# Copies for the weight sums, one behind every second weight load, and accumulating transfers head by head

## The chip, the cores and the metric

The kernel runs on one core of a Trainium2 chip. The metric is device time in microseconds (us) of one execution, the median of several. Engines are named as in the profile: PE (TensorE, matmuls), PEld (its weight loads), DVE (VectorE), ACT (ScalarE), POOL (GpSimd) and SP (SyncE, which issues DMAs). DMAs issued by POOL run in the queue q0, those of SP in q1.

## The reference

A layer of a model: 512 rows of 1024, float32. After a norm, one wide product (`w_in`) makes the inputs of two branches. Branch A (8 heads) is a gated delta rule with a convolution ahead of it; branch B (4 heads) is a retention with a rotary embedding. Both end in a norm, a gate and a product, are mixed and added, and a two-layer network of width 4096 follows.

```python
def hybrid_layer(x, ...):
    proj = rmsnorm(x, n_mix_pre) @ w_in
    qa, ka, va, za, beta_logit, a_dt, qb, kb, vb, gb, gate_a, gate_b = _split_cols(proj, IN_SIZES)
    ...
    oa = chunk_gated_delta_rule(qa, ka, va, beta, g)
    ya = (rmsnorm(oa, norm_a) * silu(za)) @ w_br_a
    qb, kb = rotary(qb), rotary(kb) * B_DK ** -0.5
    ob = chunk_retention(qb, kb, vb)
    yb = (rmsnorm(ob, norm_b) * silu(gb)) @ w_br_b
    x = x + rmsnorm((sigmoid(gate_a) * ya + sigmoid(gate_b) * yb) @ w_out, n_mix_post)
    return x + rmsnorm(square(relu(rmsnorm(x, n_mlp_pre) @ w_up)) @ w_down, n_mlp_post)
```

For each of the four heads of branch B, `vb` and `gb` are 512 columns each of `w_in`.

## The kernel before

Every float32 product is made of three matmuls: each operand is split into a high part and the rest (`mm3`). Weights come in chunks of 128 x 1024 (512 KB). A chunk is loaded by SP into a buffer `raw`, ACT writes its high part `whi` (L104), DVE the rest `wlo` (L105), and PE uses both in 24 matmuls of 128x512. `raw` has two buffers, `whi` and `wlo` three each. `weights` (L85) counts all loads in `loads`; chunk i takes its buffer from `raw_pools[i % len(raw_pools)]`. So SP can issue a load only when the split of an earlier chunk has freed its buffer, and all loads are in one queue, in the order that the scheduler laid down. Each engine works its instructions off in order; a scheduler lays that order down when the kernel is built, by priorities, and `tc.issue_after(x)` puts what is issued under it behind x.

The stages that matter here:

- Branch A: in the pools `pa` and `pa2`, a loop over `g2` (four pairs of heads). Each turn has `recurrence` (a chain of small products, with its `vn` on ACT, L637), `values_queries` for the next pair, `gated`, the partial product `ya_partial` of the pair before, and `gated_features`, which transposes the rows `vt` on PE (L211) and splits them on ACT and DVE (`og`, L194, L195).
- Branch B: in the pool `pb`, a loop over the heads h. `scores(h)` has the Q and K products, the rotary embedding (`rope`, `ro`, `qr`, `kr`) and the scores with a decay table `dec`; `outputs(h)` computes values and gates (`values_and_gates`). In the turn h = 0 the sums of the inputs (`feature_sums`: `full`, `xsum`), `ya_partial(3)` and the gate of branch A stand between the two. `pb`'s tiles lie in memory that `pa2` had used, so the first use of each waits until `pa2`'s users are done.
- `values_and_gates` makes two products with common inputs out of seven quarter products instead of eight. For that it needs four sums of blocks of `w_in` for each head, 128 x 4 x 512 each. They are made in DRAM, ahead of time, by DMAs: `BlockSums` copies four blocks of 1 MB into four tiles `sums` (L121) and then adds to each of them with accumulating DMAs of 512 KB (L127). Two of the four sums have another one as their addend, so these accumulates must wait for it. For this SP later loads 8 chunks per head from `sums` (L136).

Before the change `vg_pair` (L702) issues all of this on POOL's queue for two heads at a time, in the turns `g2` = 1 and 2, behind POOL's last instruction of that turn (`pool_marks`): 8 copies, then 16 accumulates, of which those of the third block go first. The extra `raw` buffers `ych` in `pb` (L915) come into use ahead of head 0, so that load 61, the first of the two for head 0's Q, is the first to use one.

Of the kernel before, what the change touches and what calls it, by code (L numbers as in the profile page):

```python
# [15 lines left out]
ALU = mybir.AluOpType  # L16
# [10 lines left out]
OFF_QB, OFF_KB, OFF_VB, OFF_GB = 6160, 7184, 8208, 10256  # L27
# [33 lines left out]
def hybrid_block_kernel(ctx: ExitStack, tc: tile.TileContext, a: dict, out: bass.AP):  # L61
    nc = tc.nc
    x_d = a["x"][0]
    w_in = a["w_in"][0]
# [4 lines left out]
    ring = ctx.enter_context(tc.tile_pool(name="ring", bufs=3))  # L69
    raw_pools = [(ring, "raw")]  # L70
    loads = itertools.count()
    act = ctx.enter_context(tc.tile_pool(name="act", bufs=2))
    sm = ctx.enter_context(tc.tile_pool(name="sm", bufs=2))
    psm = ctx.enter_context(tc.tile_pool(name="psm", bufs=4, space=PSUM))
# [10 lines left out]
    def weights(src, k0, nk, c0, ncols, keep=None):  # L85

        n = nk * ncols
        i = next(loads)
        pool, tag = raw_pools[i % len(raw_pools)]
        raw = pool.tile([P, 1024], F32, tag=tag, name="raw", bufs=2)  # L90
        nc.sync.dma_start(
            raw[:, :n].rearrange("p (k c) -> p k c", k=nk),
            src[k0 * P : (k0 + nk) * P, c0 : c0 + ncols].rearrange("(k p) c -> p k c", p=P),
        )
        return split_weights(raw, n, nk, keep, 200 if i >= 6 else 0)

    def split_weights(raw, n, nk, keep=None, ahead=200):
# [13 lines left out]
    class BlockSums:  # L111


        def __init__(self, src, c1, c2, tag):
            def block(kh, c):
                return src[4 * kh * P : 4 * (kh + 1) * P, c : c + 512].rearrange("(k p) c -> p k c", p=P)

            self.w12, self.first = block(0, c2), [block(0, c1), block(0, c1), block(1, c2), block(1, c1)]
            self.t = [dr.tile([P, 4, 512], F32, tag=f"{tag}{i}", name="sums", bufs=1) for i in range(4)]
            for t, b in zip(self.t, self.first):  # L120
                nc.gpsimd.dma_start(t, b)  # L121

        def add(self, i):

            src = (self.w12, self.t[2], self.w12, self.t[1])[i]
            for k in range(0, 4, 2):
                nc.gpsimd.dma_start(self.t[i][:, k : k + 2, :], src[:, k : k + 2, :], accum_op=ALU.add)  # L127

        def weights(self, i, ks):
            return block_weights(self.t[i - 1][:, 2 * ks : 2 * ks + 2, :])  # L130
# [306 lines left out]
    with tc.tile_pool(name="pa", bufs=1) as pa:  # L437
# [250 lines left out]
        def gated(g2, rows, pool):  # L688
            pss = token_major(w_in, x_tile, OFF_ZA + g2 * 512, 8)
            zz = pool.tile([P, 4, T], F32, tag="zz", name="zz")  # L690
            gate_rows(pss, rows, lambda t: zz[:, t, :])

        with tc.tile_pool(name="pa2", bufs=1) as pa2:
            keys(0, pa2)
            scr = base_inverse(0, pa2)
            vq = values_queries(0, pa2)
            keys(1, pa2)
            double_blocks(pa2, scr, 0)
            og = None
            vg_sums = []  # L700

            def vg_pair(h0):  # L702
                pair = [BlockSums(w_in, OFF_VB + h * 512, OFF_GB + h * 512, f"vg{h}") for h in range(h0, h0 + 2)]
                for i in (2, 0, 1, 3):
                    for sums in pair:
                        sums.add(i)
                return pair

            for g2 in range(4):
                rows = recurrence(g2, vq, pa2)  # L710
                if g2 == 0:
                    double_blocks(pa2, scr, 8)
                    scr = base_inverse(1, pa2)
                if g2 < 3:
                    vq = values_queries(g2 + 1, pa2)
                if g2 == 1:
                    double_blocks(pa2, scr, 16)
                    double_blocks(pa2, scr, 24)
                if g2 in (1, 2):
                    with tc.issue_after(pool_marks[-1].ins):  # L720
                        vg_sums += vg_pair(2 * g2 - 2)
                gated(g2, rows, pa2)
                if g2:
                    ya_partial(g2 - 1, og)
                og = gated_features(rows, lambda f: na[:, f % 2 : f % 2 + 1])
# [3 lines left out]
    with tc.tile_pool(name="pb", bufs=1) as pb_:  # L729
# [112 lines left out]

        def scores(h):
            dec = pb_.tile([P, T], F32, tag="dec", name="dec")
            nc.gpsimd.dma_start(dec, a["c_decay"][h])
            qs, ks = (pb_.tile([P, 2, 2, T], F32R, tag=nm, name=nm) for nm in ("qr", "kr"))
            qs, ks = [qs[:, 0], qs[:, 1]], [ks[:, 0], ks[:, 1]]
            rotary(feature_major(w_in, xs, OFF_QB + h * 256, 256, 8), qs)
            rotary(feature_major(w_in, xs, OFF_KB + h * 256, 256, 8), ks)
            scs = []  # L850
            for i in range(4):
                t0 = min(i * P, 256)
                n = T - t0
                ps = psx.tile([P, T], F32, tag="dl", name="dl", bufs=3)
                for kk in range(2):
                    mm3(
                        ps[:, :n],
                        [ks[j][:, kk, i * P : (i + 1) * P] for j in range(2)],
                        [qs[j][:, kk, t0:T] for j in range(2)],
                        kk == 0,  # L860
                        kk == 1,
                    )
                n2 = T - i * P
                sc = tmp("sc")
                nc.vector.tensor_tensor(sc[:, :n2], ps[:, n - n2 : n], dec[:, :n2], ALU.mult)
                sh, sl = (pb_.tile([P, n2], F32R, tag=f"s{i}{j}", name="s") for j in range(2))
                nc.scalar.copy(sh, sc[:, :n2])
                nc.vector.tensor_tensor(sl, sc[:, :n2], sh, ALU.subtract)
                scs.append((sh, sl))
            return scs  # L870
# [41 lines left out]
        def gate_product(off, half):  # L912
            return feature_major(w_in, xs, off + half * 512, 512, 8)

        raw_pools.append((pb_, "ych"))  # L915
        for h in range(4):
            scs = scores(h)
            if h == 0:
                feature_sums()
                ya_partial(3, prev)  # L920
                for half in range(2):
                    pss = gate_product(OFF_GA, half)
                    for f in range(4):
                        ta = tmp("g_t")
                        nc.scalar.activation(ta, pss[f], AF.Tanh, scale=0.5)
                        dst = acc[:, half * 4 + f, :]
                        nc.vector.scalar_tensor_tensor(dst, ta, 1.0, dst, ALU.add, ALU.mult)
                    nc.gpsimd.dma_start(ya_d[:, half * 4 : half * 4 + 4, :], acc[:, half * 4 : half * 4 + 4, :])
            else:
                for half, pss in branch_partial(w_br[1], prev, 4 * (h - 1)):  # L930
                    for f in range(4):
                        dst = accb[:, half * 4 + f, :]
                        if h == 1:
                            nc.scalar.copy(dst, pss[f])
                        else:
                            nc.vector.tensor_tensor(dst, dst, pss[f], ALU.add)
            rows = outputs(h, scs)
            prev = gated_features(rows, lambda f: nb[:, 4 * h + f : 4 * h + f + 1])

# [214 lines left out]
```

## Time and profile before

| | us |
|---|---|
| time, median of 3 runs | 1421.01 (1420.75 to 1422.48) |
| profiled execution, its own time | 1422.03 |
| its span, first to last instruction | 1420.3 |
| DVE busy | 869.8 |
| ACT busy | 613.2 |
| POOL busy | 98.9 |
| mean granted PE clock | 0.987 |

The profile is of one execution. A busy time is the union of an engine's instructions. Matmuls overlap, so that one of 0.39 us starts every 0.23 us; PE's share of the span says how long it had something in work. In the views of waits and of the timeline, brackets give the idle time of an engine ahead of an instruction and what ended it. "DMA share" is the mean busy share of the 16 DMA engines, "PEclk" the granted clock.

| DMA, kind | count | KB each | median us to landing |
|---|---|---|---|
| raw<-in_w_in_dram (SP) | 105 | 512 | 3.8 |
| raw<-in_w_br_a_dram (SP) | 16 | 512 | 6.4 |
| sums<-in_w_in_dram, copies (POOL) | 16 | 1024 | 19.6 |
| sums<-in_w_in_dram, accumulates (POOL) | 16 | 512 | 21.8 |
| sums<-sums, accumulates (POOL) | 16 | 512 | 16.9 |

### The profile page before, as it was taken

The page shows a single profiled execution, that of the slowest core. Times are in us where ns is not written, and L with a number is a line of the kernel's source. Part 1 is how long each engine was busy: PE and PEld are TensorE (multiplying, and loading weights), DVE is VectorE, ACT ScalarE, POOL GpSimd, SP SyncE. Part 2 cuts the span into 40 slices and gives each one's busy share as a digit, 9 for nine tenths or more (in the row PEclk, how much of TensorE's full clock was granted, in tenths as well). Part 3 has the DMA queues.
Part 4 walks back from the last instruction along what each step waited for, and adds up shares of the span by engine and source line. Part 5 has one row for each costly group of instructions (what it writes and reads, how often), then busy time and mean ns, then how long its engine had stood idle before and what let it go on. Part 6 is the DMA issues. An engine that isn't in the chain of part 4 may idle for free.

```text
span 1420.3 us, 17580 instructions
## 1 busy us (share of the span) xinstructions
PE 1376.5 (97%) x6670; PEld 1127.5 (79%) x6670; DVE 869.8 (61%) x1539; ACT 613.2 (43%) x1134; POOL 98.9 (7%) x152
## 2 busy tenths in 40 slices
PE   8999999999899979999999999999999999999997
PEld 6888787877787758887887888878788888888886
DVE  5599889843664467348467577475776324334445
ACT  6778564625443232254453353443354324132331
POOL 1111300233022000000000000000000000000000
PEclk8999999999999989999999999999999999999999
DMA  5232412289569733354262352542624323222321
GB/s 156 75 91 75 117 31 75 77 294 231 138 240 262 180 111 96 120 189 123 83 192 83 120 161 75 166 162 73 230 82 137 102 94 99 95 99 98 109 75 60
DMA packets 83959, 180.08 MB, mean 127 GB/s; under 512 B 5823, under 2 KB 19281, under 8 KB 83362
## 3 DMA queue, kind: packets, MB, share of 16 engines
q1 hardware_dynamic: 68560, 131.61, 29.6%
q0 software_dynamic: 14592, 46.10, 12.6%
q8 instruction: 52, 0.85, 0.2%
q10 hardware_dynamic: 722, 1.25, 0.2%
q14 instruction: 33, 0.27, 0.1%
HBM read 173.17 MB, written 39.32 MB: 150 GB/s over the span
## 4 chain that ended last, share of the span: by engine, by line
PE 80%; DVE 8%; DMA 8%; ACT 3%; issue 1%; SPq 0%; DVEq 0%; POOL 0%; ACTq 0%
PE mm L81 19%; PE mm L83 19%; PE mm L82 19%; PE mm L772 9%; DMA raw<-in_w_in_dram 5%; PE tr L211 2%; DVE wlo L105 2%; DMA raw<-in_w_br_a_dram 2%; PE dl L772 2%; ACT whi L104 1%; DVE c_y L399 1%; PE dl L81 1%; PE dl L83 1%; PE dl L82 1%; PE dl L662 1%
## 5 line engine op out<-in xcount | busy, mean ns | idle before, releaser
L105 DVE TENSOR_TENSOR wlo<-raw,whi 128x1024 fp32r<-128x1024 f32 x232 | 283.6, 1224 | 358.0 <-ACT whi L104 357.0
L104 ACT CAST whi<-raw 128x1024 fp32r<-128x1024 f32 x232 | 243.8, 1052 | 466.1 <-PE mm L82 206.6
L81 PE MATMUL mm<-actT,whi 128*128 128x512 f32 (+1 forms) x528 | 209.2, 397 | 8.5 <-ACT whi L104 5.1
L82 PE MATMUL mm<-actT,whi 128*128 128x512 f32 (+1 forms) x528 | 210.1, 398 | 1.0 <-DVE actT L245 1.0
L83 PE MATMUL mm<-actT,wlo 128*128 128x512 f32 (+1 forms) x528 | 209.5, 397 | 0.0
L81 PEld LDWEIGHTS mm<-actT,whi 128*128 128x128 f32 x528 | 101.3, 192 | 29.9 <-ACT whi L104 5.5
L82 PEld LDWEIGHTS mm<-actT,whi 128*128 128x128 f32 x528 | 101.6, 192 | 20.7 <-DVE actT L245 1.3
L83 PEld LDWEIGHTS mm<-actT,wlo 128*128 128x128 f32 x528 | 101.6, 192 | 19.1 <-DVE wlo L105 0.2
L81 PE MATMUL mm<-hn,whi 128*128 128x512 f32 (+1 forms) x288 | 105.6, 367 | 0.6 <-DVE r L1077 0.5
L82 PE MATMUL mm<-hn,whi 128*128 128x512 f32 (+1 forms) x288 | 105.4, 366 | 0.0
L83 PE MATMUL mm<-hn,wlo 128*128 128x512 f32 (+1 forms) x288 | 105.1, 366 | 0.0
L81 PE MATMUL mm<-og,whi 128*128 128x512 f32 x256 | 100.2, 392 | 3.0 <-DVE zz L362 3.0
L82 PE MATMUL mm<-og,whi 128*128 128x512 f32 x256 | 99.7, 389 | 0.0
L83 PE MATMUL mm<-og,wlo 128*128 128x512 f32 x256 | 99.6, 389 | 0.0
L81 PE MATMUL mm<-whi,actT 128*128 128x512 f32 x216 | 86.3, 399 | 0.1
L82 PE MATMUL mm<-wlo,actT 128*128 128x512 f32 x216 | 85.8, 397 | 0.0
L83 PE MATMUL mm<-whi,actT 128*128 128x512 f32 x216 | 85.5, 397 | 0.0
L772 PE MATMUL mm<-whi,xsum 128*128 128x512 f32 x256 | 80.1, 389 | 0.0
L399 DVE SCALAR_TENSOR_TENSOR c_y<-c_raw,convw,c_y 128x512 f32<-128x512 f32 x96 | 70.6, 753 | 2.9 <-ACT c_y L397 2.3
L81 PEld LDWEIGHTS mm<-hn,whi 128*128 128x128 f32 x288 | 54.3, 188 | 10.2 <-DVE r L1077 0.8
L82 PEld LDWEIGHTS mm<-hn,whi 128*128 128x128 f32 x288 | 54.3, 189 | 8.7
L83 PEld LDWEIGHTS mm<-hn,wlo 128*128 128x128 f32 x288 | 54.2, 189 | 8.7
(320 smaller groups left out, 2474.3 us busy)
## 6 DMA issues: line engine op xcount, KB each, us to landing
raw<-in_w_in_dram SPq DMA_DIRECT2D x105, 512.0 KB, 3.8
raw<-in_w_up_dram SPq DMA_DIRECT2D x36, 512.0 KB, 3.7
sums<-in_w_in_dram POOLq DMA_DIRECT2D x16, 1024.0 KB, 19.6
raw<-sums SPq DMA_DIRECT2D x32, 512.0 KB, 3.5
raw<-in_w_down_dram SPq DMA_DIRECT2D x32, 512.0 KB, 3.7
raw<-in_w_br_a_dram SPq DMA_DIRECT2D x16, 512.0 KB, 6.4
sums<-in_w_in_dram POOLq DMA_DIRECT2D x16, 512.0 KB, 21.8
sums<-sums POOLq DMA_DIRECT2D x16, 512.0 KB, 16.9
```

The source lines that it names most:

```text
L81: nc.tensor.matmul(ps, lh, rh, start=first, stop=False)
L82: nc.tensor.matmul(ps, lh, rl, start=False, stop=False)
L83: nc.tensor.matmul(ps, ll, rh, start=False, stop=last)
L104: nc.scalar.copy(hi[:, :n], raw[:, :n])
L105: nc.vector.tensor_tensor(lo[:, :n], raw[:, :n], hi[:, :n], ALU.subtract)
L211: nc.tensor.transpose(ps, src, ident)
L399: nc.vector.scalar_tensor_tensor(y, raw[:, j : j + T], tap(j), y, ALU.mult, ALU.add)
L662: nc.tensor.matmul(po[:, hh, :], at[:, 4 * hh + c, :], vn[:, hh, :], start=True, stop=True)
L772: m = nc.tensor.matmul(pss[t], lhs[i // 2], rhs[i % 2], start=first and k + i == 0, stop=k + i == 5, skip_group_check=not first,)
```

## The change

The copies are cut in half (512 KB, 32 of them), and go to SP's queue: `BlockSums` only lists them in `trickle`, and `weights` takes one from the list behind every second load, from load 13 on. The list has the heads in order, so that head 0's eight copies are out after load 27, head 1's after 43, head 2's after 59 and head 3's after 75. The accumulates go head by head: those of heads 0 and 1 where `vg_pair` stood (turns 1 and 2), those of heads 2 and 3 in branch B, on POOL's queue behind the `dec` load of heads 1 and 2. The `ych` buffers come into use only behind the gate of branch A in turn h = 0. What is computed stays the same.

```diff
@@ weights
-        nc.sync.dma_start(
+        load = nc.sync.dma_start(
             raw[:, :n].rearrange("p (k c) -> p k c", k=nk),
             src[k0 * P : (k0 + nk) * P, c0 : c0 + ncols].rearrange("(k p) c -> p k c", p=P),
         )
+        if i >= 13 and i % 2 and trickle:
+            sums, part, k = trickle.pop(0)
+            with tc.issue_after(load.ins):
+                sums.copy(part, k)
@@ BlockSums
-            for t, b in zip(self.t, self.first):
-                nc.gpsimd.dma_start(t, b)
-
-        def add(self, i):
-
-            src = (self.w12, self.t[2], self.w12, self.t[1])[i]
-            for k in range(0, 4, 2):
-                nc.gpsimd.dma_start(self.t[i][:, k : k + 2, :], src[:, k : k + 2, :], accum_op=ALU.add)
+            trickle.extend((self, i, k) for i in (2, 1, 3, 0) for k in (0, 2))
+
+        def copy(self, i, k):
+            nc.sync.dma_start(self.t[i][:, k : k + 2, :], self.first[i][:, k : k + 2, :])
+
+        def add(self):
+
+            for i in (2, 1, 3, 0):
+                src = (self.w12, self.t[2], self.w12, self.t[1])[i]
+                for k in range(0, 4, 2):
+                    nc.gpsimd.dma_start(self.t[i][:, k : k + 2, :], src[:, k : k + 2, :], accum_op=ALU.add)
@@ branch A
+        vg_sums = [BlockSums(w_in, OFF_VB + h * 512, OFF_GB + h * 512, f"vg{h}") for h in range(4)]
...
-                        vg_sums += vg_pair(2 * g2 - 2)
+                        vg_sums[g2 - 1].add()
@@ scores
-            nc.gpsimd.dma_start(dec, a["c_decay"][h])
+            decay = nc.gpsimd.dma_start(dec, a["c_decay"][h])
+            if h in (1, 2):
+                with tc.issue_after(decay.ins):
+                    vg_sums[h + 1].add()
@@ branch B
-        raw_pools.append((pb_, "ych"))
         for h in range(4):
             scs = scores(h)
...
+            if h == 0:
+                raw_pools.append((pb_, "ych"))
             rows = outputs(h, scs)
```

How the order of the instructions moves, at three places. In the changed kernel the lines up to L118 stand 1 to 5 lower and the later ones of branch A 8 lower.

On POOL, in the turn `g2` = 1 (behind the last `rn` load), before:

```order
L529 DMA rn<-scr 32x8x32 x3
L121 DMA sums<-in_w_in_dram 512x1x512 x8
L127 DMA sums<-in_w_in_dram 128x2x512 x8
L127 DMA sums<-sums 128x1024 x8
L389 MEMSET c_raw 128x3 x4
```

and now:

```order
L537 DMA rn<-scr 32x8x32 x3
L135 DMA sums<-in_w_in_dram 128x2x512 x3
L135 DMA sums<-sums 128x1024 x2
L135 DMA sums<-in_w_in_dram 128x2x512
L135 DMA sums<-sums 128x1024 x2
L397 MEMSET c_raw 128x3 x4
```

The copies are gone, and of 16 accumulates 8 are left, those of one head. The same 8 rows stand behind the second and the third `dec` load in branch B, ahead of the two `ya_d` stores the first time.

On SP, where branch A ends and head 0's Q and K loads (128x4x256) begin, with what each waits for, before:

```order
L91 DMA raw<-in_w_br_a_dram 128x2x512 [waits DMAHW0_49,DVE_49]
L91 DMA raw<-in_w_in_dram 128x4x256 [waits DMAHW1_49,DVE_49]
L91 DMA raw<-in_w_in_dram 128x4x256 [waits DMAHW2_49,DVE_49]
L91 DMA raw<-in_w_in_dram 128x4x256 [waits DMASW3_49,DMASW4_49,DMASW2_49,DMASW5_49,DMASW1_49,DMASW6_49,DMASW0_49,DMASW7_49,PE_49,Pool_49]
L91 DMA raw<-in_w_in_dram 128x4x256
L91 DMA raw<-in_w_br_a_dram 128x2x512 [waits DMAHW5_49,DVE_49]
```

and now:

```order
L92 DMA raw<-in_w_in_dram 128x4x256 [waits DMAHW3_49,DMAHW0_49,DVE_49]
L128 DMA sums<-in_w_in_dram 128x2x512
L92 DMA raw<-in_w_in_dram 128x4x256 [waits DMAHW2_49,DVE_49]
L92 DMA raw<-in_w_in_dram 128x4x256 [waits DMAHW6_49,DMAHW3_49,DVE_49]
L128 DMA sums<-in_w_in_dram 128x2x512
L92 DMA raw<-in_w_in_dram 128x4x256 [waits DMAHW5_49,DVE_49]
L92 DMA raw<-in_w_br_a_dram 128x2x512 [waits DMAHW6_49,DMAHW1_49,DVE_49]
L128 DMA sums<-in_w_in_dram 128x2x512
L92 DMA raw<-in_w_in_dram 128x2x512 [waits DMASW3_49,DMASW4_49,DMASW2_49,DMASW5_49,DMASW1_49,DMASW6_49,DMASW0_49,DMASW7_49,PE_49,Pool_49]
L92 DMA raw<-in_w_br_a_dram 128x2x512 [waits DMAHW4_49,DMAHW0_49,DVE_49]
```

The load that waits for PE and POOL is the first one into `ych`. Before, the order has the second load of Q and the second of K, which go to `raw`, ahead of it, and the row that waits is load 61, Q's first, followed by K's first. Now Q and K are loaded in turn, each odd load has a copy behind it, and the row that waits is a load for head 0's outputs, one load into `ya_partial(3)`.

On PE and DVE at the same place. PE before had the four groups of transposes of the last `gated_features` in one piece:

```order
L83 MATMUL mm<-og,wlo 128x512
L211 MATMUL tr<-cmat,vt 128x128 x16
L81 MATMUL mm<-actT,whi 128x512
L82 MATMUL mm<-actT,whi 128x512
L81 MATMUL mm<-actT,whi 128x512
```

and now has matmuls of head 0's Q between them; these rows are the stretch from the second to the third group:

```order
L219 MATMUL tr<-cmat,vt 128x128 x4
L84 MATMUL mm<-actT,wlo 128x512
L82 MATMUL mm<-actT,whi 128x512
L83 MATMUL mm<-actT,whi 128x512
L84 MATMUL mm<-actT,wlo 128x512
L82 MATMUL mm<-actT,whi 128x512
L83 MATMUL mm<-actT,whi 128x512
L84 MATMUL mm<-actT,wlo 128x512
L82 MATMUL mm<-actT,whi 128x512
L219 MATMUL tr<-cmat,vt 128x128 x4
```

Between the first and the second group stand 11 such matmuls, between the third and the fourth 8. DVE before had most of `full` and `xsum` ahead of the rotary embedding; the rows behind Q's last step (`qr`) read now:

```order
L110 TENSOR_TENSOR wlo<-raw,whi 128x1024
L750 TENSOR_TENSOR full<-actT 128x1024
L833 TENSOR_TENSOR ro<-mm,rope 128x512
L834 TENSOR_TENSOR ro<-mm,rope 128x512
L751 TENSOR_TENSOR full<-full 128x1024
L835 TENSOR_TENSOR ro<-mm,rope 128x512
L110 TENSOR_TENSOR wlo<-raw,whi 128x1024
L836 TENSOR_TENSOR ro<-mm,rope 128x512
L837 TENSOR_TENSOR ro<-ro 128x512
L838 TENSOR_TENSOR ro<-ro 128x512
L752 TENSOR_TENSOR full<-full 128x1024
L841 TENSOR_TENSOR kr<-ro,kr 128x512 x2
```

`full` has moved from ahead of the rotary embedding into it, and `xsum` behind it, among the scores.

More of the change, by code (lines that the diff above doesn't have):

```diff
@@ L71, in hybrid_block_kernel @@
     loads = itertools.count()
+    trickle = []
     act = ctx.enter_context(tc.tile_pool(name="act", bufs=2))
@@ L699, in hybrid_block_kernel @@
             og = None
[L700 to L707, printed above, removed]
             for g2 in range(4):
```

## The prediction

> **What bounds the kernel now.** I read the page first, then stretches of the trace, then the waits inside the bad stretches.
>
> ```profile
> PE 1376.5 (97%) x6670; PEld 1127.5 (79%) x6670; DVE 869.8 (61%) x1539; ACT 613.2 (43%) x1134; POOL 98.9 (7%) x152
> ```
>
> TensorE is the bound, with 1420.3 - 1376.5 = 43.8 us of the span not busy. The table by stretches says where these lie.
>
> ```profile
> core 0: us, PE busy (x) PEld busy (x) DVE busy (x) ACT busy (x) POOL busy (x), PEclk, DMA share, GB/s
> 95.00:288.00 193.00, 191.16 (x1182) 154.46 (x1181) 174.32 (x442) 118.42 (x315) 33.54 (x59) 1.00 0.27 74
> 288.00:372.00 84.00, 78.95 (x441) 63.47 (x439) 33.38 (x62) 28.72 (x56) 21.77 (x24) 1.00 1.00 258
> 402.00:486.00 84.00, 79.09 (x352) 63.30 (x350) 43.50 (x85) 27.98 (x53) 22.39 (x25) 1.00 1.02 269
> 505.00:542.50 37.50, 27.75 (x115) 21.92 (x113) 30.31 (x33) 14.34 (x17) 1.15 (x2) 0.82 0.41 133
> 542.50:997.00 454.50, 452.85 (x2049) 373.18 (x2048) 286.78 (x410) 188.40 (x260) 3.85 (x7) 1.00 0.40 126
> ```
>
> In two stretches of 84 us the 16 DMA engines are full (share 1.00 and 1.02). A third, 505 to 542, has a lower clock. Quiet stretches lose under 1%. The TensorE rows with idle time ahead of them (in brackets, with what ended it) name each loss:
>
> ```profile
> 333.49 0.70 PE L642 MATMUL dl<-vn,kd 128*128 128x256 f32 x2 [2.95 <-ACT vn L637]
> 373.25 0.80 PE L81 MATMUL mm<-actT,whi 128*128 128x512 f32 x1 [2.86 <-ACT c_y L397]
> 442.84 1.13 PE L642 MATMUL dl<-vn,kd 128*128 128x256 f32 x4 [3.17 <-ACT vn L637]
> 487.26 0.50 PE L81 MATMUL mm<-og,whi 128*128 128x512 f32 x1 [1.63 <-DVE zz L362]
> 507.24 0.66 PE L211 MATMUL tr<-cmat,vt 128*128 128x128 f32 x4 [1.57 <-DVE og L195]
> 509.46 0.82 PE L211 MATMUL tr<-cmat,vt 128*128 128x128 f32 x4 [1.56 <-DVE og L195]
> 511.85 1.12 PE L211 MATMUL tr<-cmat,vt 128*128 128x128 f32 x4 [1.57 <-DVE og L195]
> 518.02 0.80 PE L81 MATMUL mm<-actT,whi 128*128 128x512 f32 x1 [5.06 <-ACT whi L104]
> ```
>
> Behind the first four stands a late weight load. The chain that ended last, in order of time, has these loads (start, length):
>
> ```profile
> 321.57 9.29 DMA raw<-in_w_in_dram
> 356.47 14.53 DMA raw<-in_w_in_dram
> 431.45 9.25 DMA raw<-in_w_in_dram
> 471.68 12.52 DMA raw<-in_w_br_a_dram
> ```
>
> The first landed at 330.86, and ScalarE, which works in order, stood before it:
>
> ```profile
> 330.96 1.04 ACT L104 CAST whi<-raw 128x1024 fp32r<-128x1024 f32 x1 [2.76 <-DMA raw<-in_w_in_dram]
> 332.97 0.84 ACT L637 ACTIVATE vn<-dl,br 128x256 f32<-128x256 f32 x2
> ```
>
> So TensorE lost 2.95 us not for want of weights but because the recurrence's vn was queued on ScalarE behind a weight split. From issue to landing the weight loads (tile raw) take 10.2 us (median) in 288 to 372, the first row, and 3.7 in 100 to 288, the second:
>
> ```profile
> DMA to landing us min/median/max: 9.3/10.2/14.5
> DMA to landing us min/median/max: 3.6/3.7/4.8
> ```
>
> **The burst, now and after the change.** What fills the engines is GpSimd's queue:
>
> ```profile
> 287.99 5.90 POOL L121 DMA_DIRECT2D sums<-in_w_in_dram  x8
> 319.15 6.91 POOL L127 DMA_DIRECT2D sums<-in_w_in_dram  x6 [14.19 <-DMA sums<-in_w_in_dram]
> 354.14 0.81 POOL L127 DMA_DIRECT2D sums<-sums  x1 [1.54 <-DMA sums<-sums]
> 356.65 0.81 POOL L127 DMA_DIRECT2D sums<-sums  x1 [1.69 <-DMA sums<-sums]
> 359.50 0.81 POOL L127 DMA_DIRECT2D sums<-sums  x1 [2.04 <-DMA sums<-sums]
> ```
>
> Eight copies of 1 MB, two heads' worth, are issued from 288 on. The accumulates at 319.15 had to wait for the second head's third block, the seventh copy: (319.15 - 287.99) / 7 = 4.45 us per copy beside weight loads, 2.2 us per half. Each of the last accumulates waits for the landing of an earlier one: (359.50 - 354.14) / 2 = 2.7 us apart. The change leaves in each burst one head's 8 accumulates: 8 x 2.7 = 21.4 us. The weight loads and SP copies of that time (about four and two, 2.2 us each at most) add 13. So a burst ends about 34 us after it began, near 322 instead of 372, and the second near 436 instead of 486. The load that stalls TensorE at 330 is issued at 321.57, and the one of 356.47 is well past the end; likewise 431.45 (nearly) and 471.68.
>
> **Term 1, the bursts.** Idle in the first: 2.95 + 2.86 = 5.81 us, and a lower clock after the second of these:
>
> ```profile
> 330.00:333.50 3.50, 0.55 (x4) 0.12 (x2) 1.47 (x2) 2.54 (x5) 0.81 (x1) 1.00 1.11 238
> 373.00:376.00 3.00, 2.75 (x7) 2.18 (x8) 2.96 (x5) 2.20 (x4) 0.00 (x0) 0.55 0.49 129
> 518.00:521.50 3.50, 3.48 (x8) 2.76 (x9) 2.62 (x3) 1.64 (x2) 0.00 (x0) 0.50 0.64 215
> 521.50:525.00 3.50, 3.50 (x13) 2.74 (x13) 3.11 (x3) 1.07 (x2) 0.00 (x0) 0.72 0.76 265
> ```
>
> 3.0 us at 0.55 lose 1.35. In the second burst 3.17 + 1.63 = 4.80. Together 12.0. Bounds: all of it goes, or none, if accumulates alone slow the loads as much as copies did. I take 12.0, since three of the four late loads are issued past the new ends and the fourth, at 431.45, in the last 5 us of one.
>
> **Term 2, the late buffer.** SP's longest wait was 21.3 us, a weight load for TensorE's last transposes of the first stage; GpSimd's rope load waited for the same:
>
> ```profile
> SPq L91 <- PE tr L211: 21.3, 1, 21.3
> 513.65 0.59 POOL L731 DMA_DIRECT2D rope<-in_c_rope_dram  x1 [39.48 <-PE tr L211]
> rope<-in_c_rope_dram POOLq DMA_DIRECT2D x1, 512.0 KB, 5.3
> ```
>
> It was head 0's first Q load, into the extra buffer ych, whose memory the former stage releases only then. With ych in use from head 0's outputs on, the Q loads go to the ring, the splits are done before the transposes, and 11, 8 and 8 matmuls stand between the transposes. The three waits of 1.57 and the 5.06 go (9.76), and the clock's losses after it, 3.5 x 0.5 = 1.75 and 3.5 x 0.28 = 0.98: 12.5 in all. What is late next is VectorE. The rope table still waits for the transposes, now ended near 513, and took 5.3 us: it lands near 518.5. From there VectorE's new order has to the end of kr: 12 ro, 4 qr and kr, 3 wlo, 4 full. The first two rows price them, and the third TensorE's matmuls, 27.20 / 120 = 0.227 us each:
>
> ```profile
> 529.94 0.68 DVE L833 TENSOR_TENSOR ro<-mm,rope 128x512 f32<-128x512 f32 x1
> 528.80 1.22 DVE L754 TENSOR_TENSOR full<-full 128x1024 f32<-128x1024 f32 x1
> 611.83 27.20 PE mm L772 x120
> ```
>
> A narrow one costs at most 0.68, a wide one 1.22; queued, the end of one lies under the start of the next by some 0.08 (528.80 + 1.22 against 529.94), so 16 x 0.6 + 7 x 1.14 = 17.6 us: kr is ready near 536. TensorE gets there earlier: from 505 on it has 4 groups of transposes (0.66 each, above), 96 matmuls for Q and K and 19 for the next product: 505 + 2.6 + 115 x 0.227 = 533.7. It waits some 2.5 us and, say half the time, loses a further 1.75 of clock: 3.4, which I round to 3.5. Term 2 is 12.5 - 3.5 = 9.0, between 4 (rope lands 4 to 5 us later, beside two loads and a copy) and 12.5.
>
> On the clock: the wait at 330 left it at 1.00, that at 370, as long, took it to 0.55. The Trainium skill, "TensorE: Matmul & The Clock Gate", section "What's actually happening", says the gate halves the clock after an idle window of about 3.4 us, and that the window runs freely. The two rows agree, as the same wait fell differently. By that rule, a wait for kr beyond a window would certainly cost the drop, and the sum would be about 1 us worse than mine, 1403.5.
>
> **Costs.** (a) 32 copies on SP, each behind an odd load. The trace has no copy within DRAM issued by SP; I price it as half of one of GpSimd's, 2.2 us, between nothing (it fits into the pauses) and the slowest landing above, 14.53. In 95 to 288 (DMA share 0.27) some 12 copies add 12 x 2.2 = 26 us to 193, so the share goes to 0.41, that of the quiet stretch after 542 (0.40). A load behind a copy lands up to 2.2 later. Cover: the rows of idle time have one direct wait for weights, at 518, so TensorE has its weights in stock; without that cover each copy costs its 2.2. I take 1 us; bounds 0 and 32 x 2.2 = 70. (b) Head 2's accumulates now start behind the decay load of head 1, so near 540 (551.69 below, less the gain), beside the ring's two buffers only; loads of 10 us for 34 us could make the splits late.
>
> ```profile
> 551.69 0.55 POOL L845 DMA_DIRECT2D dec<-in_c_decay_dram  x1 [36.88 <-DVE sc L865]
> 593.09 0.55 POOL L928 DMA_DIRECT2D ya_d<-acc  x1 [40.85 <-DVE acc L927]
> ```
>
> The new wait on GpSimd holds only ya_d behind it, which is issued 41 us later: free. The first burst ran from 288 to 330 before anything was lost, with the same two buffers; this one is over in 34. I take 0.5, bounds 0 and 6 (one burst's idle). Head 3's burst falls where four buffers serve: 0, at most the same 6.
>
> **Sum.** 12.0 + 9.0 - 1 - 0.5 = 19.5 us off. The profiled execution took 1422.0 (span 1420.3), 1.0 over the median 1421.0 of the runs shown. 1422.0 - 19.5 = **1402.5**.
>
> **Rivals.**
> - *The accumulates alone choke the loads.* For: the slowest load, 14.53 us from 356.47, ran beside accumulates of sums alone. Against: the burst is over before the loads that hurt. Then term 1 is near 3: 1422 - 3 - 9 + 1.5 = 1411.5. Chance 0.14.
> - *VectorE takes the place of the buffer wait.* For: it is busy 30.3 of 37.5 us already and must do this in 10 us less. Term 2 falls to 2-4: 1422 - 12 - 3 + 1.5 = 1408.5. Chance 0.11.
> - *Slower: copies in the loads' own queue.* Before, copies and loads were in two queues; now a load waits behind a copy wherever it is issued within 2 us of it, and the landing of 4.8 against a median of 3.7 in the quiet stretch shows that even two loads close together pay. If 32 copies cost TensorE more than 20.5 / 32 = 0.64 us each (12.0 + 9.0 - 0.5 being gained), the change loses; at 1 us each it takes 1422 - 20.5 + 32 = 1433.5. Against: the stock of weights, above. Chance 0.05. The Trainium skill, "DMA: Bandwidth & Descriptors", section "Queues, rings and completion order", has descriptors of one ring consumed in order, rings of different queues served in turn: by it the load pays a copy's whole 2.2 us, and this rival's condition holds at every close pair; it leaves open whether TensorE notices.
> - *It does not do what it says:* copies bunch up where SP stands (it still waits for the transposes, now at a later load), accumulates wait for them, and the stalls move: about 1421. Chance 0.04.
> - *More:* no wait for kr and both bursts harmless: 1393 to 1396. Chance 0.08.
>
> **Numbers.** The forecast (1398 to 1408) has 0.58. A measurement can tell about 0.2%, 2.8 us, from no change. Faster: 0.58 + 0.08 + 0.14 + 0.11 = 0.91; same 0.04; slower 0.05. The range runs from the best case to past the first rival: 1393 to 1414. It leaves out the slower and the unchanged case and the tails of the others, under two tenths.
>
> **What would show it.** Right: the DMA share of 288 to 372 near 0.6, full for about 34 us; no wait of vn over 1 us; no wait of SP for the transposes that TensorE feels, clock 1.00 near 520, a wait of 2 to 5 us at the scores of head 0. Wrong: idle rows again near 330 and 440, loads of over 6 us between 95 and 288, idle near 560 to 600, or a missing wait for kr.

## The result, and the profile after

| | before | after |
|---|---|---|
| median of 6 runs each, us | 1421.74 | 1410.69 |
| lowest to highest, us | 1418.15 to 1425.24 | 1407.90 to 1413.27 |
| profiled execution, us (span) | 1422.03 (1420.3) | 1413.15 (1411.4) |

The ratio is 0.9921, with a 95% interval of 0.9899 to 0.9943: 11 us faster by the medians, 8.9 by the two profiled executions. The forecast was 1402.5, a gain of 19.5 us; the time lies in the range (1393 to 1414), but about half of the gain is missing.

The page's first line after the change:

```profile
PE 1378.8 (98%) x6670; PEld 1128.3 (80%) x6670; DVE 868.5 (62%) x1539; ACT 613.5 (43%) x1134; POOL 87.7 (6%) x136
```

The table by stretches, with the two of before that carried the argument (95 to 288 and 288 to 372) and short ones around TensorE's new losses (length, busy time of each engine, granted clock, DMA share, GB/s):

```profile
95.00:288.00 193.00, 191.24 (x1183) 154.60 (x1182) 173.79 (x440) 117.68 (x312) 34.37 (x60) 1.00 0.34 104
288.00:325.00 37.00, 33.95 (x234) 27.02 (x233) 15.43 (x24) 9.49 (x13) 7.22 (x8) 0.99 0.98 199
288.00:372.00 84.00, 80.95 (x443) 65.13 (x442) 38.15 (x68) 32.63 (x62) 7.22 (x8) 0.98 0.61 145
322.90:328.00 5.10, 5.10 (x15) 4.05 (x16) 0.87 (x2) 1.24 (x2) 0.00 (x0) 0.67 0.76 253
424.90:428.50 3.60, 3.59 (x9) 2.83 (x10) 1.66 (x3) 0.91 (x1) 0.00 (x0) 0.50 1.06 251
520.00:539.00 19.00, 18.01 (x85) 14.79 (x84) 19.00 (x27) 8.95 (x12) 0.76 (x2) 1.00 0.38 127
544.00:547.50 3.50, 3.50 (x9) 2.73 (x10) 1.58 (x3) 0.00 (x0) 0.86 (x1) 0.50 1.07 169
```

The change does what it says: the engines are full for 37 us instead of 84, and the share over 288 to 372 is 0.61. But the timeline of TensorE still has rows with idle time ahead of them (what the engine waited for is in brackets). They stand in other places:

```profile
322.89 0.50 PE L82 MATMUL mm<-og,whi 128*128 128x512 f32 x1 [3.05 <-ACT acc L441]
424.91 0.76 PE L82 MATMUL mm<-og,whi 128*128 128x512 f32 x1 [4.18 <-DVE acc L443]
528.66 0.50 PE L82 MATMUL dl<-qr,kr 128*128 128x512 f32 x1 [0.75 <-ACT kr L840]
543.84 0.80 PE L82 MATMUL mm<-og,whi 128*128 128x512 f32 x1 [4.43 <-DVE acc L443]
719.50 0.50 PE L772 MATMUL mm<-whi,xsum 128*128 128x512 f32 x1 [1.59 <-ACT p L814]
```

The waits for vn (2.95 and 3.17 before), for og (three of 1.57) and for whi (5.06) are gone. Three waits of 3 to 4.4 us for `acc` have come. That is the evacuation of a branch product (`ya_partial`): its second half needs the four PSUM banks that the first half fills, so TensorE stops until ScalarE or VectorE has emptied them. What stood ahead of `acc` is seen on those engines' timelines. ScalarE, at the first wait:

```profile
314.65 1.55 ACT L441 COPY acc<-mm 128x512 f32<-128x512 f32 x3
321.31 1.04 ACT L109 CAST whi<-raw 128x1024 fp32r<-128x1024 f32 x1 [5.11 <-DMA raw<-in_w_in_dram]
322.26 0.58 ACT L441 COPY acc<-mm 128x512 f32<-128x512 f32 x1
```

VectorE, at the second and the third:

```profile
413.59 0.88 DVE L372 SCALAR_TENSOR_TENSOR vt<-vt,rstd,zz 128x256 f32<-128x256 f32 x2
422.94 1.23 DVE L110 TENSOR_TENSOR wlo<-raw,whi 128x1024 fp32r<-128x1024 f32 x1 [8.47 <-ACT whi L109]
424.08 2.47 DVE L443 TENSOR_TENSOR acc<-acc,mm 128x512 f32<-128x512 f32 x4
...
540.83 1.22 DVE L110 TENSOR_TENSOR wlo<-raw,whi 128x1024 fp32r<-128x1024 f32 x1
541.97 1.22 DVE L758 TENSOR_TENSOR xsum<-full,xsum 128x1024 fp32r<-128x1024 f32 x1
543.10 2.48 DVE L443 TENSOR_TENSOR acc<-acc,mm 128x512 f32<-128x512 f32 x4
```

The first two are one case: the fourth `acc` at 322.26, and all four at 424.08, are ready, and stand in an in-order queue behind the split of a weight load that has not landed. The third is another: no row ahead of 543.10 has idle time, so VectorE is simply behind with its work (the feature sums, `full` and `xsum`).

To compare whole stages I add up what TensorE lost in them: for each two neighbouring matmuls the distance of their starts, less the median distance for that shape in the trace of before. This takes in idle time and the lower clock alike. It leaves out the first 285 us and the end (from 990 on); by the same count the end scatters by up to 4 us between the profiles of all runs.

| us lost by TensorE in | 285 to 395 (head 0's burst) | 395 to 495 (head 1's) | 495 to 600 (late buffer; head 2's) | 660 to 740 (head 3's) |
|---|---|---|---|---|
| before | 13.3 | 8.9 | 12.7 | -0.2 |
| after | 9.0 | 8.0 | 7.8 | 0.9 |

The four differences sum to 9.0 us. The stretch left out between them, 600 to 660, went from 0.0 to 0.8 lost, so 8.2 of the 8.9 us of the profiled executions are accounted for.

### The profile page after: what moved, and what is told of

The parts are those of the page before. It is cut to its first block, busy times and chain, and to the rows that moved or that the text cites. A ratio compares the mean times of both kernels' runs of the same rounds, so it can differ in the third digit from the quotient of the medians.

```text
span 1411.4 us, 17607 instructions
## 1 busy us (share of the span) xinstructions
PE 1378.8 (98%) x6670; PEld 1128.3 (80%) x6670; DVE 868.5 (62%) x1539; ACT 613.5 (43%) x1134; POOL 87.7 (6%) x136
## 4 chain that ended last, share of the span: by engine, by line
PE 57%; DVE 3%; DMA 1%; ACT 1%; issue 1%; DVEq 0%; ACTq 0%; SPq 0%
PE mm L82 14%; PE mm L84 14%; PE mm L83 14%; PE mm L772 9%; PE dl L772 2%; PE dl L82 1%; PE dl L84 1%; PE dl L83 1%; PE tr L219 1%; DMA raw<-in_w_out_dram 1%; DVE wlo L110 0%; ACT whi L109 0%; DVE tb L966 0%; DVE actT L968 0%; DVE tb L965 0%
## 5 line engine op out<-in xcount | busy, mean ns | idle before, releaser
L83 PEld LDWEIGHTS mm<-actT,whi 128*128 128x128 f32 x528 | 100.3, 190 | 20.3 <-DVE actT L253 1.3
L82 PE MATMUL mm<-og,whi 128*128 128x512 f32 x256 | 102.9, 402 | 11.9 <-DVE acc L443 8.6
L83 PE MATMUL mm<-og,whi 128*128 128x512 f32 x256 | 102.2, 399 | 0.0
L82 PEld LDWEIGHTS mm<-og,whi 128*128 128x128 f32 x256 | 49.7, 194 | 24.1 <-DVE acc L443 4.8
L82 PEld LDWEIGHTS mm<-hn,whi 128*128 128x128 f32 x288 | 54.3, 189 | 10.1 <-DVE r L1081 0.8
```

The costliest lines, as they stand in the source:

```text
L82: nc.tensor.matmul(ps, lh, rh, start=first, stop=False)
L83: nc.tensor.matmul(ps, lh, rl, start=False, stop=False)
```

## Experiments

Each run was compared with runs of the kernel before on the same chip. Ratios are to that kernel, with their 95% intervals; the last columns are the losses of the table above. They come from one profile each. A half-clock stretch of 3.4 us costs 1.7 us, and whether one follows a wait varies (the last section has a pair), so a difference of under 2 us between two rows says little.

| run | median us | ratio | lost 285 to 395 | 395 to 495 | 495 to 600 | 600 to 660 | 660 to 740 |
|---|---|---|---|---|---|---|---|
| e1, late buffer only | 1415.81 | 0.9968 (0.9955 to 0.9980) | 14.5 | 10.0 | 8.5 | 0.0 | -0.2 |
| e2, copies moved, two of them late | 1413.50 | 0.9954 (0.9938 to 0.9970) | 7.7 | 15.0 | 7.7 | 0.7 | -0.8 |
| e3, copies without accumulates | 1396.59 | 0.9831 (0.9818 to 0.9845) | 4.8 | 1.3 | 7.0 | 0.9 | -0.3 |
| e4, sums behind the product | 1410.51 | 0.9928 (0.9915 to 0.9941) | 9.2 | 7.0 | 7.3 | 0.8 | 2.7 |
| e5, copies outside the bursts | 1404.26 | 0.9882 (0.9865 to 0.9900) | 8.9 | 3.7 | 8.5 | 0.8 | -0.5 |
| e6, e4 and two bursts later | 1404.99 | 0.9890 (0.9874 to 0.9905) | 7.3 | 6.8 | 0.3 | 0.9 | 3.1 |
| e7, accumulates in a chain | 1404.57 | 0.9890 (0.9869 to 0.9912) | 10.2 | 1.1 | 7.3 | 0.9 | 1.1 |
| e8, banks first | 1403.45 | 0.9883 (0.9860 to 0.9906) | 5.0 | 4.2 | 6.5 | 0.9 | 2.9 |
| e9, e5 and e6 | 1399.14 | 0.9845 (0.9819 to 0.9871) | 7.5 | 5.9 | 1.0 | 0.9 | 0.1 |
| e10, e9 and e7 | 1400.46 | 0.9847 (0.9814 to 0.9880) | 6.2 | 1.2 | 0.9 | 0.2 | 1.8 |
| e11, e9 and e8 | 1392.97 | 0.9804 (0.9774 to 0.9834) | 4.7 | 2.0 | 0.9 | 1.0 | 0.1 |
| e12, e9, head 1's burst near 600 | 1409.83 | 0.9920 (0.9893 to 0.9948) | 6.8 | 1.2 | 1.6 | 14.5 | 0.7 |

### e1: the late buffer alone

```diff
-        raw_pools.append((pb_, "ych"))
         for h in range(4):
...
+            if h == 0:
+                raw_pools.append((pb_, "ych"))
             rows = outputs(h, scs)
```

> The kernel before with one part of the change alone: ych comes into use from head 0's outputs on. Three theories. (V) VectorE becomes the bound behind it: the 13.8 us that TensorE lost in 500 to 530 go, but the feature sums, which are done later for the same rope table, hold the evacuation of the last branch product (acc), and some 6.5 to 8 come back between 530 and 550: 5 to 7 us off, 1415 to 1417. (F) The forecast's term is right: 9.0 off, 1412.7. (A) The stall at 539 in the changed kernel is made by head 2's accumulates, which start at 538.8 there and are not present here: 12 off, 1409.5.

Measured: 1415.8, theory V. The long wait is there, at the same two operations as after the whole change, with no accumulate anywhere near. TensorE's row, then VectorE's timeline:

```profile
553.44 0.80 PE L81 MATMUL mm<-og,whi 128*128 128x512 f32 x1 [4.41 <-DVE acc L435]
```

```profile
550.43 1.23 DVE L105 TENSOR_TENSOR wlo<-raw,whi 128x1024 fp32r<-128x1024 f32 x1
551.56 1.23 DVE L758 TENSOR_TENSOR xsum<-full,xsum 128x1024 fp32r<-128x1024 f32 x1
552.70 2.48 DVE L435 TENSOR_TENSOR acc<-acc,mm 128x512 f32<-128x512 f32 x4
```

So the late buffer saves 12.7 - 8.5 = 4.2 us in its stage, not 9.

### e2 and e5: copies away from the bursts

```diff
-        if i >= 13 and i % 2 and trickle:
+        if i >= 11 and i % 2 and not (36 <= i <= 42 or 49 <= i <= 56 or 72 <= i <= 78) and trickle:   # e2
+        if (13 <= i < 28 and i % 2 or 28 <= i < 36 or i >= 57 and i % 2 and not 72 <= i <= 78) and trickle:   # e5
```

> The changed kernel, but no copy is issued behind the loads that fall into the first three bursts of accumulates (36 to 42, 49 to 56, 72 to 78); the copies start one odd load earlier and the others follow later. (C) The copies, in the loads' own queue, make the late loads of the bursts: those loads land in 6 to 8 us instead of 10 to 15, the waits at 319 (3.2 us and 1.7 of clock) and 420 (4.4 and 2.4) shrink to under 1 us each: 1400 to 1404. (A) The accumulates alone do it: the loads still take 9 us and more, the waits stay within 1 us of what they were, 1408.5 to 1412.

e2 (1413.5) says nothing on this. Two half copies of head 1, behind loads 45 and 47, came later in the program than head 1's accumulates, so those sums lack addends, and SP, with the weight loads behind it, waited for the accumulates ("SPq L128" waited 20.3 us in 380 to 460). That would explain the 15.0 us in 395 to 495; it was not tested by itself. e5 has all copies ahead of their accumulates.

> The changed kernel, but no copy is issued in the first three bursts: heads 0 and 1 have theirs behind the odd loads 13 to 27 and every load 28 to 35, head 2 behind odd loads 57 to 71, head 3 from 79 on; all of them still ahead of their accumulates. (A) Accumulates alone hold the loads: loads in the bursts still take 9 us and more, the waits at 319 and 420 stay within 1.5 us: 1408.5 to 1412. (C) The copies in the loads' queue have a part in it: loads in 6 to 8 us, waits under 1 us each: 1400 to 1404.

Measured: 1404.3, the time of C with half the picture of A. In the first burst nothing changed much: loads 9.9 us (median; 10.6 after the change), 8.9 us lost. (Other runs agree: 7.7 in e2 and 7.5 in e9, without copies there too, 9.2 in e4 and 7.3 in e6, with them.) In the second, loads fell from 11.3 to 9.7, the slowest from 15.1 to 11.4, and the loss from 8.0 to 3.7. The weight loads of 288 to 325 and of 402 to 432, after the change:

```profile
DMA to landing us min/median/max: 4.4/10.6/13.7
...
DMA to landing us min/median/max: 4.3/11.3/15.1
```

The same in e5, and TensorE's row that answers to 424.91:

```profile
DMA to landing us min/median/max: 3.9/9.9/12.9
...
DMA to landing us min/median/max: 6.5/9.7/11.4
```

```profile
421.58 0.47 PE L82 MATMUL mm<-og,whi 128*128 128x512 f32 x1 [0.58 <-DVE acc L443]
```

After the change SP issues a copy at 413.40, right behind the load of 412.99 that took 14.5 us. So copies beside the accumulates cost something in the second burst and next to nothing in the first, though the DMA engines were full in both; why the two differ isn't shown. In the second, the load that the split waited for landed at 418.4 instead of 421.8, and a wait of 4.18 us shrank to 0.58: what a microsecond of lateness costs depends on which side of the need it falls. Of e5's 6.4 us, 1.4 are in 660 to 740, where the kernel after issues no copy and e5 one, at 670, ahead of head 3's burst; I can't say why.

### e3: copies without accumulates

```diff
-                    nc.gpsimd.dma_start(self.t[i][:, k : k + 2, :], src[:, k : k + 2, :], accum_op=ALU.add)
+                    pass
```

> The changed kernel with all 32 accumulates left out (so the sums hold only their first addend); the copies stay. (A) The waits at 319, 420 and 717 go, with their clock: 3.2 + 1.7 + 4.4 + 2.4 + 1.8 = 13.5 off, near 1397, and the 6.5 us between 530 and 550 stay, since VectorE makes them; the copies then cost nothing that shows. (C) If copies hold the loads, loads beside copies still take over 6 us in the former bursts and at most half of that goes: 1404 and more. If the accumulates make the stall at 539 as well: 1391.

Measured: 1396.6, theory A to the microsecond. Two stretches of its table, which in the kernel before had 78.95 and 79.09 of 84 us busy, and the landing of its weight loads in 288 to 325 and in 402 to 432:

```profile
288.00:372.00 84.00, 83.41 (x463) 67.31 (x461) 41.85 (x73) 35.12 (x65) 0.36 (x3) 1.00 0.32 97
402.00:486.00 84.00, 84.00 (x380) 68.88 (x379) 48.49 (x83) 29.41 (x54) 0.00 (x0) 1.00 0.37 115
```

```profile
DMA to landing us min/median/max: 3.6/3.7/4.3
...
DMA to landing us min/median/max: 3.6/3.8/4.0
```

With no accumulate beside them the 32 copies cost nothing that shows, and the loads are as quick as in quiet stretches. The 7.0 us of 495 to 600 stay: they are not the bursts'.

### e4 and e6: VectorE's backlog, and what it covered

```diff
-                feature_sums()
                 ya_partial(3, prev)
+                feature_sums()
...
-            if h in (1, 2):          # e6 only
+            if h in (2, 3):
                 with tc.issue_after(decay.ins):
-                    vg_sums[h + 1].add()
+                    vg_sums[h].add()
```

> The changed kernel, with the feature sums written behind the last branch product, so that in VectorE's order four xsum and one weight split come behind the first four acc instead of ahead of them. (V) The wait at 539 (4.6 us, and some 2 of clock) is VectorE's queue: it goes, 5 to 6.5 off, 1404 to 1406, unless the sums are late for the products at 603. (A) It is made by the accumulates or by late weights: the wait stays over 3 us, 1409 to 1412.

Measured: 1410.5, no change, and yet V holds: the wait at 539 is gone. TensorE meets another, as long, 33 us later. Its row, and ScalarE's timeline there:

```profile
576.76 0.79 PE L82 MATMUL mm<-actT,whi 128*128 128x512 f32 x1 [4.45 <-ACT g_t L927]
```

```profile
563.05 1.05 ACT L109 CAST whi<-raw 128x1024 fp32r<-128x1024 f32 x1 [9.39 <-DMA raw<-in_w_in_dram]
568.47 1.05 ACT L109 CAST whi<-raw 128x1024 fp32r<-128x1024 f32 x1 [4.38 <-DMA raw<-in_w_in_dram]
575.17 1.04 ACT L109 CAST whi<-raw 128x1024 fp32r<-128x1024 f32 x1 [5.65 <-DMA raw<-in_w_in_dram]
576.12 1.57 ACT L927 ACTIVATE g_t<-mm 128x512 f32<-128x512 f32 x3
```

That is head 2's burst: again an evacuation behind splits that wait for loads. The load that ends the last of these waits lands at 575.1, and at 575.3 after the change; there the wait for VectorE had put TensorE 4 us back, so that it got there no earlier than the work it needed, and its timeline has no idle time in 565 to 580. Two causes stood one behind the other, and taking one away uncovers the other.

> As e4 (feature sums behind the last branch product), and the accumulates of heads 2 and 3 one head later (behind the decay load of heads 2 and 3), where the weight loads have four buffers. (V and A) In e4 the wait of 4.6 us moved from 539 to 572, where head 2's burst held the loads; with the burst gone from there it goes: 6 us off e4, 1404 to 1406, with 1.9 us lost at each of the two late bursts. If VectorE's backlog makes another wait by itself between 530 and 600, 1409 and more.

Measured: 1405.0, as V and A together have it: 0.3 us lost in 495 to 600. The two late bursts cost 3.1 us in 660 to 740 and 2.5 in 740 to 990 (0.6 before).

### e7: fewer accumulates in flight

```diff
-            for i in (2, 1, 3, 0):
+            last = None
+            for k, i in ((0, 2), (0, 1), (0, 0), (0, 3), (2, 2), (2, 1), (2, 0), (2, 3)):
                 src = (self.w12, self.t[2], self.w12, self.t[1])[i]
-                for k in range(0, 4, 2):
-                    nc.gpsimd.dma_start(self.t[i][:, k : k + 2, :], src[:, k : k + 2, :], accum_op=ALU.add)
+                with tc.issue_after(last.ins) if last else nullcontext():
+                    last = nc.gpsimd.dma_start(self.t[i][:, k : k + 2, :], src[:, k : k + 2, :], accum_op=ALU.add)
```

> The changed kernel with each head's accumulates issued in the order of a chain (half by half; every other one waits for the landing of the one ahead), so that at most two are in flight instead of three or four. Bytes are the same. (D) The number in flight holds the loads: they land in 5 to 9 us instead of 8 to 15, the bursts take 40 us and more, the waits at 319 and 420 fall below 1.5 us: 1401 to 1405. (A) The bytes do it: loads as late as before over the same or a longer stretch, 1409 to 1413.

Measured: 1404.6, the time of D, but not in both places. Weight loads in 288 to 325 and 402 to 432, and the longest wait of the first burst:

```profile
DMA to landing us min/median/max: 5.9/8.7/12.4
...
DMA to landing us min/median/max: 4.5/7.9/9.9
```

```profile
334.24 0.70 PE L650 MATMUL dl<-vn,kd 128*128 128x256 f32 x2 [4.23 <-ACT vn L645]
```

The loads are quicker, and the second burst costs next to nothing (1.1 us). But the first now lasts from 287.8 to 335.6, 48 us instead of 38, and so reaches the `vn` that already stalled the kernel before at 330. A gentler burst is a longer one.

### e8: the banks first

```diff
-        with tc.high_priority(ahead):
+        with tc.high_priority(ahead), held.pop() if held else nullcontext():
...
                 if g2 == 0:
-                    nc.scalar.copy(dst, pss[f])
+                    m = nc.scalar.copy(dst, pss[f])
                 else:
-                    nc.vector.tensor_tensor(dst, dst, pss[f], ALU.add)
+                    m = nc.vector.tensor_tensor(dst, dst, pss[f], ALU.add)
+            held[:] = [tc.issue_after(m.ins), nullcontext()]
```

> The changed kernel with the second weight split behind each evacuation of a branch product held back until the four acc are done, on the engine that makes them (ScalarE for the first product, VectorE later). (O) At 319 and 420 TensorE has weights in stock and lacks PSUM banks only because acc stands behind a split that waits for a late load: the waits of 3.2 and 4.4 us go, 6 to 10 off, 1401 to 1405. (W) The weights themselves are late: the waits come back within 10 us as waits for whi, 1409 and more.

Measured: 1403.5. In 285 to 395 theory O holds (9.0 to 5.0 lost, e3's 4.8 without any burst). In 395 to 495 a wait of 2.62 us for `vn` takes the place of that of 4.18. VectorE's timeline at the second wait, where the order is now the other way round:

```profile
416.79 0.69 DVE L443 TENSOR_TENSOR acc<-acc,mm 128x512 f32<-128x512 f32 x1 [0.67 <-PE mm L84]
418.15 0.69 DVE L443 TENSOR_TENSOR acc<-acc,mm 128x512 f32<-128x512 f32 x1 [0.67 <-PE mm L84]
419.28 1.23 DVE L110 TENSOR_TENSOR wlo<-raw,whi 128x1024 fp32r<-128x1024 f32 x1 [0.44 <-ACT whi L109]
```

Each bank is emptied as soon as TensorE is done with it, and the weights come in time, though the loads are as late as before (9.5 to 14.2 us). One reservation: the order forced here also moved other work of these stages, so not all of the gain need be the banks'.

### e9 to e12: putting them together

e9 is e6 with the copies of e5 (for loads from 57 on every odd one); e10 is e9 with the chain of e7; e11 is e9 with e8; e12 is e9 with

```diff
-                if g2 in (1, 2):
+                if g2 == 1:
...
+                    stored = nc.gpsimd.dma_start(ya_d[:, half * 4 : half * 4 + 4, :], acc[:, half * 4 : half * 4 + 4, :])
+                with tc.issue_after(stored.ins):
+                    vg_sums[1].add()
```

> e6 (feature sums behind the product, the accumulates of heads 2 and 3 one head later) with the copies of heads 0 and 1 out of the bursts, as in e5. If the causes add: e5 lost 3.0 us around 420 where e6 lost 5.7, and 0.4 at the late burst where e6 lost 2.0 and more, so 4 to 5 off e6's 1405.0: 1400 to 1401.5. If what e5 gained was the place of head 3's burst or chance, not the copies: 1404 to 1406.

> e9 with the accumulates in a chain, as in e7. The second burst's loss falls from 3 us to about 1; the first burst, 48 us long in e7, still reaches the vn of 330 and loses 4 to 6 there, as against 4 in e9: 1399 to 1401. If only bytes count: as e9.

> e9 with the second weight split behind the acc evacuation, as in e8. The bank waits at 320 and 420 go (4 us and 1 to 3): 1396 to 1399, unless a wait for vn near 430 (3.4 us in e8) takes their place: 1399 to 1401.

> e9 with head 1's accumulates behind the store of ya_d (near 600), in the four-buffer stage, so that only head 0's burst is left in the two-buffer stage. The 1 to 3 us at 420 go and some 2 come for the new burst: 1399 to 1402. If the loads between 604 and 640, which follow each other every 2 to 3 us, can't bear a burst: a wait of over 4 us there, 1403 to 1408.

e9 (1399.1) came out a microsecond better than the sum of the parts, mostly in 660 to 740 (0.1 against e6's 3.1); in 395 to 495 it lost 5.9, not e5's 3.7. The wait for `acc` of 424.91 is gone there as in e5, but one of 2.54 us for `og` follows at 434.71, with half clock behind it; in e5 that one was 1.52 us, at full clock. e10 (1400.5) can't be told from e9, though its table shows less lost in both bursts; one of its four runs took 1394.4, the profiled one.

e11 (1393.0, ratio 0.9804) beats both kernels: no wait of TensorE in it is longer than 1.6 us. The first three of its list of waits (us in total, times, longest):

```profile
PE tr L219 <- DVE o L910: 1.6, 4, 0.4
PE dl L82 <- ACT kr L840: 1.6, 1, 1.6
PE dl L269 <- DVE warm L264: 1.5, 1, 1.5
```

e12 (1409.8) is worse than expected by both its cases. The burst, 590 to 632, falls on weight loads that follow each other every 2 to 3 us; those issued from 600 on took 8.9 to 22.3 us, and TensorE ran dry:

```profile
632.21 0.80 PE L772 MATMUL mm<-whi,xsum 128*128 128x512 f32 x1 [8.88 <-ACT whi L109]
```

So four buffers do not make a burst harmless. The number of loads in it doesn't explain that: ten are issued within this burst, and ten within head 3's after the change (680 to 719), which lost 0.9 us. What this one has besides is three copies of SP among the loads (17.3 us to landing in the median) and a store of 1 MB; no run takes these away, so the cause stays open.

## Why the prediction was half right

**Direction and range: right; the sum of the terms, 19.5 us, was about twice the gain.** The change does what was foretold of it: a DMA share of 0.61 (near 0.6 foretold), full for 37 us (34), no wait for `vn`, a clock of 1.00 in 520 to 539, no load over 6 us in the quiet stretch. The wait for `kr` came too, but as 0.75 us, not 2 to 5. And one sign of being wrong came: idle rows in the bursts, at 323 and 425 (330 and 440 were named). The forecast's own band, 1398 to 1408, was missed; the time lies in the range because that was drawn past the rivals, and two of them came true in part.

**Term 1, the bursts: mis-sized, 12.0 us.** In the first two bursts 4.3 and 0.9 us were saved. The step that failed is to take from "three of the four late loads are issued past the new ends" that the loss goes with them. The ends came near their places (324.9 and 430.3; 322 and 436 foretold), but a load is not late by its place in the program: those inside the shorter burst, up to 13.7 and 15.1 us, were later than any in the same part of it before (at most 10.2), and the stall moved ahead to the next operation queued behind a split, `acc`. The bound "none, if accumulates alone slow the loads as much as copies did" was the better guess. That is the first rival, which gave 1411.5, and e3 shows its mechanism: with the accumulates out, 3.7 us per load and 14 us off. By e3, which still loses 4.8 and 1.3 us in these stages, the two bursts cost 8.5 and 7.6 us before the change, more than the 12.0 of the term.

**Term 2, the late buffer: mis-sized, 9.0 us.** The old losses went, all 12.5. The wait for `kr` that was to come, 2.5 us, is 0.75: the rope table landed at 513.2, not 518.5, as its issue came earlier too. But I let the count of VectorE's work end with `kr`. The feature sums have 12 wide operations, and six of them stand behind `kr` and ahead of `acc`. The wait is there, 4.43 us with 5.5 us at half clock behind it, 15 us later than I looked (e1, e4). The rival "VectorE takes the place" named the engine and not the place.

**Cost (a), the copies: right where it was argued, missed where it was not.** In 95 to 288 TensorE was busy 191.24 us (191.16 before), so they cost nothing there; the 1 us allowed was ample. The slower rival's mechanism, a load held up by a copy in its own queue, shows in the second burst, where taking the copies away saved 4.3 us in e5, but 0.9 in e9 against e6, since another wait came up there. In the first burst it doesn't show.

**Cost (b), head 2's burst: 0.5 us by luck.** Its own price is a wait of 4.45 us (e4), near the upper bound of 6. It did not show because VectorE's wait comes first and gives the loads their time. Head 3's burst, put at 0, cost 1.1 us by these two profiles, within what one half-clock stretch makes.

**The clock.** That the two rows agree with the rule named there holds for the chance in it: the same wait may cost clock or not. It does not hold for the length. Waits of 2.86 us (before), 3.05 (after) and 2.25 (e5) were followed by half clock, and each is shorter than the window of that rule.

**The sum by stages**: 4.3 + 0.9 + 4.9 - 1.1 = 9.0 us, less 0.8 in 600 to 660, where the forecast had 7.2 + 4.8 + 8.5 + 0 - 1 = 19.5.

## What to carry to other kernels

Find the operation that an in-order engine has queued behind each split of a late load, not only the load: here it was the evacuation of PSUM banks, and putting it ahead (e8) was worth as much as making the transfers gentler (e7). A shorter burst of transfers is not a weaker one; ask which loads fall into it now and what is queued behind them. When a wait goes, follow the engine that is next to its end (all its queued work, not up to the first consumer), and expect a second cause behind the first: e4 took a wait of 4.4 us away and gained nothing until e6 took the next.

## What the runs showed of the hardware

- Accumulating transfers within DRAM hold weight loads from another queue: with three or four of 512 KB in flight a 512 KB load takes 10.6 and 11.3 us in the median and up to 15.1 (9.9 and 9.7 with no copy beside them, e5), with two 8.7 and 7.9, without them 3.7 and 3.8 (e3). In 288 to 325 the DMA engines are full (0.98) at 199 GB/s, where GpSimd's copies and first accumulates filled them at 310 before. The Trainium skill, "DMA: Bandwidth & Descriptors", section "Queues, rings and completion order", has each DMA engine take the rings in turn; by it I'd estimate twice the quiet time, 7.4 us, which the chain of e7 comes near (7.9 and 8.7) and the plain bursts exceed.
- 32 copies of 512 KB issued by SP, within DRAM, cost nothing that shows in stretches with a DMA share of 0.32 to 0.37 (95 to 288 after the change, and e3). In the two bursts (share 0.98 and 1.05) loads took 10.6 and 11.3 us in the median with copies and 9.9 and 9.7 without (e5).
- The Trainium skill, "Perfetto Trace Analysis", section "Optimizing Tensor Performance", has independent matmul groups rotate through PSUM banks so that evacuation overlaps the next group. The kernel rotates four for these products. After the change they did not suffice: `acc` stood behind a split for which VectorE had been idle 8.47 us. With the evacuation put ahead of that split (e8) both waits for `acc` are gone, so here the rotation helps when nothing that can wait for a transfer stands ahead of the evacuation in its queue.
- Whether a wait of TensorE costs clock is in part chance. At the same matmul of the first burst, with the same order of TensorE's instructions up to there, e5 waited 2.25 us at 323.21 and had a clock of 0.50 in 324.4 to 327.7; e9 waited 2.31 us at 323.57 and had 1.00 in 323.6 to 330.
